# adaLN weights of a two-layer diffusion block: the first layer's later rounds wait for its first, and the second layer's run beside the last route

## The chip, the cores and the metric

One core of one Trainium2 chip runs the whole program. The metric is the device time of one execution in microseconds (us), the median of several runs on one chip.

## What is computed

Two layers of a hybrid attention and expert-retrieval block over 512 latent and 256 context tokens, cut to what matters here:

```python
def reference(...):
    s_c, s_cctx = silu(c), silu(c_ctx)
    h_lat, h_ctx = x, ctx                       # 512 and 256 tokens of 1024
    for l in range(2):
        mod = (s_c @ ada_w[l] + ada_b[l]).reshape(1, 6, 1024)
        sh1, sc1, g1, sh2, sc2, g2 = mod
        mod_c = (s_cctx @ ada_w[l] + ada_b[l]).reshape(6, 1024)
        a_lat = rms_norm(h_lat, norm1_g[l]) * (1 + sc1) + sh1
        a_ctx = rms_norm(h_ctx, norm1_g[l]) * (1 + mod_c[1]) + mod_c[0]
        p_lat, p_ctx = a_lat @ w_in[l], a_ctx @ w_in[l]
        o_mla, o_swa = latent attention over ctx and latent keys, windowed attention with sinks
        h_lat = h_lat + g1 * (concat(o_mla, o_swa) @ w_out[l])
        # (layer 0 only: the same for the ctx tokens, which see ctx alone, with mod_c[2])
        b = rms_norm(h, norm2_g[l]) * (1 + sc2) + sh2
        q = (b @ peer_wq[l]).reshape(T, 8, 2, 128);  s = q . peer_keys[l]
        # top 16 of each half, top 16 of the 256 sums: 128 experts idx[t, 8 * 16] per token, softmax g
        a = gelu(b . peer_u[l][idx])
        h = h + g2 * sum_k (g * a)[k] * peer_v[l][idx[k]]
    return h_lat
```

"adaLN" is the line that makes `mod`: two conditioning vectors (latent and context) times a 1024 x 6144 matrix for each layer, 25 MB of float32 a layer, from which come the shifts, scales and gates.

## The kernel before

**How the work is tiled.** Tokens go in tiles of 128: `("ctx", 0..1)` and `("lat", 0..3)`. Each layer has an attention part, in which generators for the steps of a tile are run one after another (`run`) or interleaved by weights (`par`: `par((a, 24), (b, 48))` takes about two steps of b for one of a), and then a dense expert part. The steps: `KV`, `Q`, `KVQ` make keys, values and queries; `A` is attention; `O` the output projection with the gate and the second norm; `R` the route (16 weight tiles `wq` of 512 KB, products L656, scores L631, top 16 by DVE L637 to L641); `G` chooses the experts; `GH` chooses and then builds one-hot tables for a dense tile (`one_hots`: DVE L852 and L863, PE L864, ACT L865, stores `Gd<-ar` from SP). Tiles that are not dense get their experts by gathered rows (`gv<-u,idx`, `gv<-v,idx` by POOL, L766; DVE L770, L780). Of the first layer, the gathers of both context tiles and of latent tile 3 are rows; 353 of these 768 rows are issued ahead of the dense part.

**What sets the order.** Outside the dense loops a scheduler orders each engine's instructions ahead of time; on the chip every engine and every DMA queue takes them strictly in that order. Two buffer pools for weights matter:

- `wts`, tag `w4`: 4 buffers of 512 KB, loaded from SP's queue. All of `w_in`, `wukv`, `w_out`, `wq`, and in the dense part `raw`, pass through them.
- `gat`, tag `gv`: 5 buffers of 512 KB, loaded from POOL's queue. The gathers use them.

**adaLN** (`ada`) takes three rounds a layer. A round loads 16 tiles of 512 KB (8 steps `k`, two tiles each), does 4 products of 2 x 512 for each step (L220, one PSUM bank), loads the bias (`ada_b`, 256 KB), adds it (4 times L226 on DVE), stores the gates of rounds 1 and 2 to memory, transposes (L232) and copies the result out. Round 0 gives `m[0]`, `m[1]` (first norm), round 1 the first gate and `m[3]`, round 2 `m[4]` and the second gate. Round 0 of the first layer uses `w4` from SP; all other rounds use `gv` from POOL and the one PSUM bank `acc` (tag `acc`, one buffer), which `one_hots` needs too (L829, L830). The first layer's three rounds are all free to start at once. The second layer's three start when the queries of context tile 1 exist (`early`), that is beside `A(ctx 1)`, `R(ctx 0)` and the latent `KV`:

```python
a = ada(l, m)
next(a)
run(KVQ(c, 0, 1))
run(a, A(c, 0), O((c, 0)))
early = qs[c, 1][1][:, 0, 0:1]
par((A(c, 1), 16), (R((c, 0)), 16))
run(G(c, 0), ada(1, mods[1], early))
...
par((R((t, 3)), 24), (GH(2, True), 48))
run(G(t, 3))
```

The functions that the diff touches:

## Time and profile before

| | us |
|---|---|
| median of 3 runs | 4384.81 |
| lowest, highest run | 4382.21, 4393.07 |
| profiled execution | 4393.17 |
| its span on the core | 4391.4 |

The profiled execution lies 8.4 us above the median, and its own time is 1.8 us more than its span. All positions below are microseconds from the start of that span. PE is TensorE (matmul), PEld its weight loads, DVE VectorE, ACT ScalarE, POOL GpSimd, SP SyncE; "SPq" and "POOLq" are queues. A fp32 product counts as two records (x8 is four products).

### The profile page before, as it was taken

What the parts mean: (1) busy time and instruction counts of PE and PEld (TensorE: products, weight loads), DVE (VectorE), ACT (ScalarE), POOL (GpSimd) and SP (SyncE); (2) the same over time, 40 slices, a digit from 0 to 9 for tenths busy, and PEclk for the clock granted to TensorE, in tenths of its full rate; (3) what the DMA queues carried; (4) which work ended last, traced back from release to release, by engine and by line L of the source; (5) the groups of instructions that cost most, each with busy time, mean ns of one, the idle gap of its engine ahead of it and who ended that gap; (6) DMA issues with size and microseconds to landing.
All of it is one profiled execution on the core that took longest, in us unless ns stands there. A gap on an engine that the chain in (4) does not pass through costs nothing.

```text
span 4391.4 us, 58196 instructions
## 1 busy us (share of the span) xinstructions
PE 3604.6 (82%) x19934; PEld 2903.4 (66%) x19934; DVE 3370.1 (77%) x7630; ACT 1658.4 (38%) x3116; POOL 1632.5 (37%) x1402
## 2 busy tenths in 40 slices
PE   6886679478786999999999678677776469999997
PEld 2453348347576899999999545444555357888886
DVE  1247778989778888888888743578889989888887
ACT  1332232146465333333333234142223554444443
POOL 2015564554200444444444510155454444222222
PEclk8997789688898999999999889888888569999999
DMA  8488898888746999999999862689899889999997
GB/s 305 161 295 295 308 336 320 299 294 320 249 166 219 352 336 336 337 354 336 336 335 316 317 223 87 212 311 365 292 341 339 279 295 394 317 322 318 319 319 245
DMA packets 471066, 1306.51 MB, mean 298 GB/s; under 512 B 45152, under 2 KB 151392, under 8 KB 470768
## 3 DMA queue, kind: packets, MB, share of 16 engines
q0 software_dynamic: 199744, 726.26, 46.6%
q1 hardware_dynamic: 271024, 576.52, 37.6%
q8 instruction: 157, 2.57, 0.2%
q14 instruction: 141, 1.16, 0.1%
HBM read 1240.70 MB, written 61.90 MB: 297 GB/s over the span
## 4 chain that ended last, share of the span: by engine, by line
PE 27%; DVE 24%; issue 22%; DMA 13%; ACT 7%; POOL 6%; POOLq 0%; ACTq 0%; SPq 0%; DVEq 0%
DVE vacc L780 6%; POOL gv L766 6%; PE m L656 4%; DVE gv L770 4%; DVE v L880 3%; PE A L943 3%; PE o L906 3%; DMA gv<-v,idx 3%; ACT u L879 3%; PE m L384 3%; DMA gv<-u,idx 2%; DMA w<-w_in 2%; PE acc L864 2%; PE big L587 1%; DMA raw<-uT 1%
## 5 line engine op out<-in xcount | busy, mean ns | idle before, releaser
L766 POOL DMA_INDIRECT gv<-v,idx x640 | 777.6, 1215 | 1105.8 <-DVE vacc L780 757.1
L766 POOL DMA_INDIRECT gv<-u,idx x640 | 792.5, 1238 | 863.2 <-DVE a L770 511.7
L943 PE MATMUL A<-b,u 128*128 128x384 f32 (+1 forms) x6144 | 960.4, 312 | 55.0 <-ACT w L946 28.2
L943 PEld LDWEIGHTS A<-b,u 128*128 128x128 f32 x6144 | 929.6, 191 | 91.7 <-ACT w L946 46.1
L906 PE MATMUL o<-v,W 128*128 128x512 f32 x3840 | 922.5, 392 | 9.5 <-ACT W L879 9.5
L780 DVE SCALAR_TENSOR_TENSOR vacc<-gv,a,vacc 128x1024 f32<-128x1024 f32 x635 | 811.5, 1278 | 54.3 <-DMA gv<-v,idx 47.0
L770 DVE CUSTOM_DVE_ANT_0 gv<-gv,btok 128x1024 f32<-128x1024 f32 x640 | 768.9, 1219 | 86.2 <-DMA gv<-u,idx 83.6
L906 PEld LDWEIGHTS o<-v,W 128*128 128x128 f32 x3840 | 713.2, 189 | 148.3 <-ACT W L879 10.0
L880 DVE TENSOR_TENSOR u<-raw,u 128x1024 fp32r<-128x1024 f32 x256 | 313.6, 1225 | 116.0 <-ACT u L879 114.0
L879 ACT ACTIVATE W<-w 128x384 fp32r<-128x384 f32 (+1 forms) x256 | 120.9, 472 | 711.9 <-DVE w L949 711.9
L384 PE MATMUL m<-w,aT 128*128 128x256 f32 (+3 forms) x672 | 256.8, 531 | 86.5 <-DMA w<-w_in 53.5
L880 DVE TENSOR_TENSOR v<-raw,v 128x1024 fp32r<-128x1024 f32 x256 | 312.2, 1219 | 17.4 <-ACT v L879 17.3
L656 PE MATMUL m<-bT,wq 128*128 128x128 f32 x2432 | 304.5, 282 | 3.1 <-DMA wq<-wq 2.5
L656 PEld LDWEIGHTS m<-bT,wq 128*128 128x128 f32 x2432 | 292.6, 199 | 7.3 <-DMA wq<-wq 3.4
L879 ACT ACTIVATE v<-raw 128x1024 fp32r<-128x1024 f32 x256 | 268.3, 1048 | 24.3 <-PE o L906 23.8
L879 ACT ACTIVATE u<-raw 128x1024 fp32r<-128x1024 f32 x256 | 267.7, 1046 | 25.5 <-DMA raw<-uT 25.3
L384 PEld LDWEIGHTS m<-w,aT 128*128 128x128 f32 x672 | 139.6, 218 | 188.9 <-DMA w<-w_in 66.6
L946 ACT ACTIVATE w<-A 128x384 f32<-128x384 f32 (+1 forms) x256 | 109.2, 426 | 354.7 <-PE A L943 354.7
L880 DVE TENSOR_TENSOR W<-w,W 128x384 fp32r<-128x384 f32 (+1 forms) x256 | 125.8, 491 | 143.7 <-ACT W L879 143.6
L516 ACT ACTIVATE peT<-m 128x512 f32<-128x512 f32 (+1 forms) x192 | 109.8, 576 | 238.3 <-PE m L519 132.3
L548 PE MATMUL big<-kT,qT 96*128 96x256 f32 (+1 forms) x288 | 135.8, 606 | 72.8 <-ACT pexp L496 35.0
L864 PE MATMUL acc<-o,o 128*128 128x128 f32 x768 | 140.1, 336 | 65.7 <-ACT ar L865 60.7
(223 smaller groups left out, 4347.8 us busy)
## 6 DMA issues: line engine op xcount, KB each, us to landing
raw<-uT SPq DMA_DIRECT2D x256, 512.0 KB, 5.5
raw<-v SPq DMA_DIRECT2D x256, 512.0 KB, 5.4
wq<-wq SPq DMA_DIRECT2D x136, 512.0 KB, 6.6
gv<-ada_w POOLq DMA_DIRECT2D x80, 512.0 KB, 6.7
Gd<-ar SPq DMA_DIRECT2D x80, 512.0 KB, 4.1
w<-w_out SPq DMA_DIRECT2D x68, 512.0 KB, 6.2
G<-Gd SPq DMA_DIRECT2D x128, 192.0 KB, 5.8
G<-Gd SPq DMA_DIRECT2D x128, 128.0 KB, 5.5
```

Of the source, the lines that this page charges most:

```text
L384: nc.tensor.matmul(ps[:, :cn], aT[:, k, :], w[k][:, :cn], start=(k == 0), stop=(k == KC - 1))
L516: nc.scalar.activation(dv, pt[:, :2 * bn * P], AF.Copy)
L548: nc.tensor.matmul(ps[:, k0:k0 + n], qT[:, h, :], kv["kT"][:, h, k0:k0 + n], start=True, stop=True)
L656: nc.tensor.matmul(ps[:, c], w[:, k, :], bT[:, k, :], start=(k == 0), stop=(k == KC - 1))
L766: return t, nc.gpsimd.indirect_dma_start(out=t, out_offset=None, in_=src, in_offset=bass.IndirectOffsetOnAxis(ap=idx[:, k:k + 1], axis=0))
L770: ins = nc.vector.tensor_tensor_reduce(out=t, in0=t, in1=bt, scale=1.0, scalar=0.0, op0=OP.mult, op1=OP.add, accum_out=a[:, k:k + 1])
L780: return nc.vector.scalar_tensor_tensor(acc, t, w[:, k:k + 1], acc, op0=OP.mult, op1=OP.add)
L864: nc.tensor.matmul(ps[:, x * NK:(x + 1) * NK], o1[:, x], o2, start=True, stop=True)
L879: nc.scalar.activation(hi, x, AF.Copy)
L880: nc.vector.tensor_tensor(lo, x, hi.bitcast(F32), OP.subtract)
L906: nc.tensor.matmul(acc[t][x], W[:, a_, c], v[:, b_, x * 512:(x + 1) * 512], start=(e == 0 and (a_, b_) == PARTS[0]), stop=(e == NK - 1 and ...
L943: nc.tensor.matmul(A, u[:, a_, k * P:(k + 1) * P], b[:, b_, k], start=(k == 0 and (a_, b_) == PARTS[0]), stop=(k == KC - 1 and (a_, b_) == ...
```

## The change

Two edits. In the first layer, the first tile of round 1 is written by a DVE copy of round 0's result (L205), so its load, and all of POOL's loads behind it, wait for round 0. The second layer's three rounds leave the place beside context route 0 and run as a third member of the last `par` of layer 0, beside the route of latent tile 3 and the one-hots of latent tile 2; their weights and biases go through `w4` from SP, and their gates are stored from ACT's queue.

```diff
--- before.py
+++ after.py
@@ -201,7 +201,7 @@
             ws = []
             for i in range(2):
                 w = gv_tile(2 * 512).rearrange("p (j n) -> p j n", j=2)
-                if after is not None and (r, k, i) == (0, 0, 0):
+                if after is not None and (k, i) == (0, 0):
                     nc.vector.tensor_copy(w[:, 0, 0:1], after)
                 nc.gpsimd.dma_start(w.rearrange("p j n -> p (j n)"),
                                     I["ada_w"][l][k * P:(k + 1) * P, (2 * r + i) * D:(2 * r + i + 1) * D])
@@ -209,24 +209,30 @@
             return ws
         return load
 
-    def ada(l, m, early=None):
+    def ada(l, m):
+
 
         for r in range(3):
-            load, ps_a, ps_t = (ada_w, mm, m1) if (l, r) == (0, 0) else (ada_w_early(early), acc_ps, acc_ps)
+            late = l > 0
+            load, ps_a, ps_t = (ada_w, mm, m1) if (l, r) == (0, 0) else \
+                (ada_w, acc_ps, acc_ps) if late else (ada_w_early(m[0][:, 0, 0:1] if r == 1 else None), acc_ps, acc_ps)
+            q = nc.sync if late else nc.gpsimd
             ps = ps_a()
             for k in range(KC):
                 w = load(l, r, k)
                 for j in range(4):
                     nc.tensor.matmul(ps[32 * j:32 * j + 2, :], sT[:, k, :], w[j],
                                      start=(k == 0), stop=(k == KC - 1))
-            rows = gv_tile(512)
-            nc.gpsimd.dma_start(rows, I["ada_b"][l, r])
+                if late:
+                    yield
+            rows = wts.tile([P, 512], F32, tag="w4", name="adab") if late else gv_tile(512)
+            q.dma_start(rows, I["ada_b"][l, r])
             for j in range(4):
                 x = rows[32 * j:32 * j + 2, :]
                 nc.vector.tensor_tensor(x, x, ps[32 * j:32 * j + 2, :], OP.add)
                 i = 2 * r + j // 2
                 if i in (2, 5):
-                    nc.gpsimd.dma_start(gates[l, i][:, (j % 2) * 512:(j % 2 + 1) * 512], x)
+                    (nc.scalar if late else q).dma_start(gates[l, i][:, (j % 2) * 512:(j % 2 + 1) * 512], x)
             pt = ps_t()
             for c in range(4):
                 nc.tensor.transpose(pt[:, c * P:(c + 1) * P], rows[:, c * P:(c + 1) * P], ident)
@@ -1083,9 +1089,8 @@
                 next(a)
                 run(KVQ(c, 0, 1))
                 run(a, A(c, 0), O((c, 0)))
-                early = qs[c, 1][1][:, 0, 0:1]
                 par((A(c, 1), 16), (R((c, 0)), 16))
-                run(G(c, 0), ada(1, mods[1], early))
+                run(G(c, 0))
                 run(KV(t, 0, 1), KV(t, 2, 3), Q(t, 0, 1), A(t, 0), O((c, 1), (t, 0)))
                 par((A(t, 1), 8), (R((c, 1), (t, 0)), 24))
                 run(G(c, 1), O((t, 1)), Q(t, 2, 3))
@@ -1093,7 +1098,7 @@
                 run(O((t, 2)))
                 par((A(t, 3), 8), (R((t, 2)), 24), (GH(1), 48))
                 run(O((t, 3)))
-                par((R((t, 3)), 24), (GH(2, True), 48))
+                par((R((t, 3)), 24), (GH(2, True), 48), (ada(1, mods[1]), 40))
                 run(G(t, 3))
             else:
                 run(KV(c, 0, 1), KV(t, 0, 1), Q(t, 0), left)
```

How it moves instructions, at three places. PE at the start (`m_136` is round 0's PSUM bank, `acc` that of the other rounds; `gv` and `adaw` are weight tiles, `sT` the conditioning vectors, `hld` a token tile). Before:

```order
L220 MATMUL acc<-gv,sT 2x512 x4
L220 MATMUL m_136<-adaw,sT 2x512 x4
L220 MATMUL acc<-gv,sT 2x512 x2
L220 MATMUL m_136<-adaw,sT 2x512 x4
L220 MATMUL acc<-gv,sT 2x512 x6
```

PE at the start now (line numbers of the changed kernel: L224 is L220, L238 is L232, L283 is L277, L390 is L384):

```order
L224 MATMUL m_136<-adaw,sT 2x512 x32
L238 MATMUL m_207<-ident,gv 128x128 x4
L283 MATMUL m_229<-diag,hld 128x128 x4
L283 MATMUL m_238<-diag,hld 128x128 x4
L390 MATMUL m_283<-w_275,aT 128x288 x2
```

Round 0's 32 products stand alone at the head; round 1's follow behind the first norm, and round 1 now ends (its L232) where round 2 ended before, round 2 some 30 us of the old timeline later, behind the query projection.

POOL's queue, from the first load to the first gathers. Before:

```order
L206 DMA gv<-ada_w 128x1024 x16
L223 DMA gv<-ada_b 128x512
L206 DMA gv<-ada_w 128x1024 x14
L796 DMA btok<-b_ctx_1151 128x1024
L206 DMA gv<-ada_w 128x1024 x2
L223 DMA gv<-ada_b 128x512
L206 DMA gv<-ada_w 128x1024 x4
L229 DMA gate_92<-gv 2x512 x2
L206 DMA gv<-ada_w 128x1024 x12
L223 DMA gv<-ada_b 128x512
L229 DMA gate_93<-gv 2x512 x2
L766 DMA gv<-u,idx 128x1024 x128
```

These are the second layer's 48 loads; the first layer's 32 stand ahead of them. Now, from the first load of all on:

```order
L229 DMA gv<-ada_b 128x512
L206 DMA gv<-ada_w 128x1024 x16
L229 DMA gv<-ada_b 128x512
L206 DMA gv<-ada_w 128x1024 x4
L235 DMA gate_90<-gv 2x512 x2
L206 DMA gv<-ada_w 128x1024 x12
L229 DMA gv<-ada_b 128x512
L235 DMA gate_91<-gv 2x512 x2
L802 DMA btok<-b_ctx_1152 128x1024
L772 DMA gv<-u,idx 128x1024 x128
```

The second layer's loads are gone from it.

SP's queue at the last route (`b_lat` is the stored second norm of tile 3, which is ready only when that norm is). Before:

```order
L182 DMA w_8011<-w_out 128x2x512
L652 DMA wq<-wq 128x1024 x4
L248 DMA gate<-gate_90 128x512
L868 DMA Gd<-ar 128x1024 x2
L152 DMA h_lat_8033<-hld 128x1024
L613 DMA b_lat_8074<-hld 128x1024
L652 DMA wq<-wq 128x1024 x4
L868 DMA Gd<-ar 128x1024
L652 DMA wq<-wq 128x1024 x3
L868 DMA Gd<-ar 128x1024
```

Now:

```order
L193 DMA adaw<-ada_w 128x1024 x2
L874 DMA Gd<-ar 128x1024
L193 DMA adaw<-ada_w 128x1024 x2
L254 DMA gate<-gate_90 128x512
L874 DMA Gd<-ar 128x1024
L152 DMA h_lat_7783<-hld 128x1024
L874 DMA Gd<-ar 128x1024
L658 DMA wq<-wq 128x1024
L193 DMA adaw<-ada_w 128x1024 x4
L619 DMA b_lat_7824<-hld 128x1024
L658 DMA wq<-wq 128x1024
L193 DMA adaw<-ada_w 128x1024 x2
```

Between one `wq` tile and the next stand two to four `adaw` tiles; 58 tiles for `w4` and 16 of the `Gd` stores follow behind `b_lat`, the last `wq` behind the last `Gd`. On PE the one-hots' first step (`acc<-ident,ef`) stands behind the 32 products of the second layer's round 0, since both use the bank `acc`.

## Rows read from the trace of the kernel before

**Rows 1.** The page, busy time of each engine over the whole span (share, instructions).

```profile
PE 3604.6 (82%) x19934; PEld 2903.4 (66%) x19934; DVE 3370.1 (77%) x7630; ACT 1658.4 (38%) x3116; POOL 1632.5 (37%) x1402
```

**Rows 2.** Stretches: PE, PEld, DVE, ACT, POOL busy (instructions); clock, DMA share, GB/s.

```profile
0.00:60.00 60.00, 34.04 (x137) 4.59 (x138) 6.10 (x21) 5.56 (x9) 11.83 (x28) 0.77 0.95 356
108.00:175.00 67.00, 50.07 (x157) 29.25 (x158) 11.89 (x29) 23.44 (x53) 0.00 (x0) 0.89 0.38 128
175.00:347.00 172.00, 148.13 (x941) 88.07 (x940) 79.50 (x399) 63.51 (x171) 27.31 (x53) 0.95 0.73 253
347.00:1240.00 893.00, 653.58 (x3646) 471.69 (x3647) 734.22 (x1994) 329.67 (x743) 431.07 (x358) 0.82 0.85 301
1275.00:1409.00 134.00, 87.79 (x624) 79.25 (x623) 107.20 (x477) 74.65 (x136) 0.57 (x1) 0.84 0.63 213
1409.00:2400.00 991.00, 988.20 (x4991) 899.81 (x4991) 845.93 (x1140) 359.44 (x484) 454.14 (x353) 1.00 0.95 336
```

**Rows 3.** The same view, line L220 alone (PE busy, PEld busy, clock, DMA).

```profile
60.00:108.00 48.00, 13.21 (x64) 1.52 (x64) 0.96 0.70 238
...
175.00:250.00 75.00, 19.02 (x100) 2.15 (x100) 0.91 0.76 258
...
175.00:347.00 172.00, 35.66 (x192) 4.11 (x192) 0.95 0.73 253
```

**Rows 4.** Timeline, start and first gather: start, duration, engine, line, tile, count [idle before].

```profile
4.34 2.09 SPq L193 DMA_DIRECT2D adaw<-ada_w  x4
...
7.16 3.62 PE L220 MATMUL acc<-gv,sT 128*2 128x512 f32 x8 [7.16 <-DMA gv<-ada_w]
...
54.36 1.69 PE L220 MATMUL m<-adaw,sT 128*2 128x512 f32 x8
...
103.88 0.66 PE L232 MATMUL acc<-ident,gv 128*128 128x128 f32 x4
...
346.97 1.07 POOL L766 DMA_INDIRECT gv<-u,idx  x1 [6.78 <-issue]
```

**Rows 5.** DMA of 0 to 60 us: GB/s in 40 slices, issues with landing time.

```profile
GB/s 0 71 239 398 409 257 280 325 413 423 418 423 414 414 395 420 416 421 418 426 415 418 426 418 421 350 281 268 232 300 396 415 426 415 421 361 225 329 358 370
...
adaw<-ada_w SPq DMA_DIRECT2D x16, 512.0 KB, 9.9
```

**Rows 6.** Chain that ended last, 175 to 250 us, by line; waits 175 to 347 us.

```profile
by line: issue 22.7%; PE big L587 19.0%; PE acc L220 14.4%; DMA gate<-gate 13.3%; DMA gv<-ada_w 11.1%; PE m L277 5.0%; PE m L519 2.4%; PE m L512 2.0%; ACT L253 1.7%; PE big L565 1.7%; DVE upd L596 1.6%; ACT upd L261 1.5%; PE big L548 1.4%; 
...
PE acc L232 <- DVE gv L226: 3.1, 1, 3.1
```

**Rows 7.** DMA of 1275 to 1409 us: packets and bytes, issues with landing time.

```profile
DMA packets 16660, 28.58 MB, mean 213 GB/s; under 512 B 1190, under 2 KB 10406, under 8 KB 16650
...
wq<-wq SPq DMA_DIRECT2D x16, 512.0 KB, 4.6
...
gate<-gate SPq DMA_DIRECT2D x1, 256.0 KB, 4.5
```

**Rows 8.** Timeline of the last route: SP's queue, then PE.

```profile
1304.24 6.58 SPq L652 DMA_DIRECT2D wq<-wq  x4
...
1327.31 4.05 SPq L652 DMA_DIRECT2D wq<-wq  x3
...
1389.71 11.57 SPq L917 DMA_DIRECT2D G<-Gd  x16
...
1299.86 0.42 PE L829 MATMUL acc<-ident,ef 128*128 128x128 f32 x1
...
1408.67 1.01 PE L943 MATMUL A<-b,u 128*128 128x384 f32 x2 [22.80 <-ACT u L879]
```

**Rows 9.** Timeline of DVE there, and line L226's durations (min/median/max ns).

```profile
1384.22 0.34 DVE L863 TENSOR_SCALAR o<-io,i,gT 128x128 f32<-128x128 f32 x1
...
1385.26 0.28 DVE L641 FIND_INDEX8 i<-v,mrep 128x8 uint32<-128x128 f32 x1
...
L226 DVE TENSOR_TENSOR gv<-gv,acc x12: 668/683/694, 218.9 to 338.7; 2x512 f32<-2x512 f32 x12
```

## The prediction

> **What bounds the kernel now.** I began with the page's busy times. No engine holds the whole span: PE has 82%, DVE 77% [rows 1]. So I cut the span into stretches and read for each which column is nearest to full [rows 2]. The reader should see six different kernels there. The dense stretch (1409 to 2400) is PE-bound, 988 of 991 us, and the change leaves its instructions alone; it moves as a block. The gather stretch (347 to 1240) has no full engine: DVE is busy 734 of 893 us and the DMA share is 0.85. The edits touch the other four: the first 60 us, where the DMA share is 0.95 and PE waits for weights; 108 to 175, where PE has 17 us idle and the DMA is at 0.38; 175 to 347, where PE is busy 148 of 172 us; and the last route, 1275 to 1409, where PE is busy 88 of 134 us, DVE 107, and the DMA share is 0.63. In the first stretch I read the timeline [rows 4] and the transfers [rows 5]; in 175 to 347 the chain and the waits [rows 6]; at the last route the transfers and the timelines [rows 7 to 9].
>
> **Part 1a: round 0 alone at the start.** Rounds 0 and 1 load together, and the last product of round 0 is at 54.4 us, ending at 56 [rows 4]. The stretch moves 356 GB/s on average, 413 to 426 in its best slices, and an `adaw` tile takes 9.9 us to land in this crowd [rows 5]. Alone, round 0 needs its 16 tiles and what else is loaded beside it (two token tiles and small tables, which I take as 3 tiles more): 19 x 0.524 = 10 MB. At 356 GB/s that is 28 us. It starts when the first tile lands: issue at 4.3 [rows 4] and, with the queue empty, about 5 us as the 4.6 of a `wq` tile in a quieter place [rows 7]. 9 + 28 = 37 us instead of 56: **-19 us**. Bounds: at 418 GB/s 24 us and an end at 33, -23; if four buffers starve and the rate falls to 300 (the 301 of the gather stretch, rows 2), 33 us and an end at 42, -14.
>
> **Part 1b: rounds 1 and 2 come later.** Round 1's first load in POOL's queue now waits for the result of round 0, and everything of POOL behind it: the other 31 tiles, the bias loads, the gate stores. That is 16 MB from about 38 us, at 356 GB/s done by 85 us, so the transfers are not late for what follows. The products are in another place, though: round 1's stand where round 2's stood (64 records, 13.2 us of PE between 60 and 108, rows 3), and round 2's 13.2 us go behind the query projection, into 108 to 175. There PE has 17 us of idle time [rows 2], but a chain of attention steps and norms goes through it, and an idle share of 25% does not hide all of it. I take two thirds, **+9 us**. Bounds: 0 if PE's idle time takes it; 20 if all 13.2 count and the bank `acc`, the adds (4 x 0.68 us, rows 9) and the gate make the second norm late by some 7 us more.
>
> **Part 2a: the second layer's rounds leave 175 to 347.** In 175 to 250 us the chain gives 14.4% of 75 us, 10.8 us, to L220 [rows 6], and L220 was busy there for 19.0 us [rows 3]: 57% of it was on the path. Of the 35.7 us in the whole stretch [rows 3] that is 20.3. The chain also has 13.3%, 10 us, on a gate load [rows 6] that takes 4.5 us where there is less traffic [rows 7]: 5.5 more. A transposition that waits 3.1 us for an add [rows 6] goes too. **-29 us**. Bounds: 9 if only the two waits go and other work fills the 35.7 us; 44 if all of it was on the path. Parts 1 and 2a together bring POOL's first gather from 347.0 [rows 4] to about 308.
>
> **Part 2b: the same work beside the last route.** It adds 48 weight tiles of 0.524 MB and three biases to a stretch that moves 28.58 MB [rows 7]: 28.6 + 26.0 = 54.5 MB. All of it and the 16 `wq` tiles go through the 4 `w4` buffers in SP's order, and 58 tiles stand behind the store `b_lat`, which waits for tile 3's second norm. What waits behind SP's waiting instruction: the route's `wq` tiles and 16 `Gd` stores. What waits behind round 0 on PE: the first step of the one-hots, which needs the bank `acc`. I cost it along that order. Before, the first `wq` behind `b_lat` goes at 1304.2 and the one-hots' first product at 1299.9 [rows 8]. Now 12 tiles of round 0 come behind `b_lat`: 12 x 1.5 us (1.5 is what a tile takes at 356 GB/s), the last lands 4.6 us after its issue [rows 7], and four adds take 2.7 [rows 9]: 1304.2 + 18 + 4.6 + 2.7 = 1329.5, so the one-hots begin about 29 us late. They took from 1299.9 [rows 8] to 1384.2 [rows 9] on a DVE that was busy 107 of 134 us [rows 2], so little of a late start is made up; eight more adds of rounds 1 and 2 put 5.5 us on it. At the end the last `wq` now stands behind the last `Gd`, and on DVE the last top-16 and the choice of tile 3 come after the last one-hot, where they were over 1 us behind it before [rows 9]: a landing of 4.6, a product and the searches, 10 us. 29 + 5.5 + 10 = **+45 us**. Read the other way this is 58 tiles at 2.0 us each: 1304 + 116 + 10 = 1430 against 1385.
>
> Bounds of this term come from the bytes. 54.5 MB take 130 us at the 418 GB/s of the best early slices [rows 5], within the old 134: +0, hidden. At 356 they take 153, +19; at 336 (the dense stretch, rows 2) 162, +28; at 301 (gathers) 181, +47. I chose a value near the last, since stores in small packets (10,406 of 16,660 under 2 KB, rows 7) and waits in one queue mix here as among the gathers, and not as at the start. PE could hold it: 87.8 + 35.7 = 123.5 us of work in 134.
>
> Rows 5 show slices of 413 to 426 GB/s for more than 20 us in a stretch of loads from memory. The Trainium skill, page "DMA: Bandwidth & Descriptors", section "Where 436 GB/s comes from", says that for transfers between memory and SBUF the memory's side, about 358 GB/s for a core, is what binds. The measurement goes above that here, so it decides for the bound of +0; by the page's figure the stage would need an estimated 152 us, +18, and the sum would be 21 us below the old time.
>
> **Sum.** -19 + 9 - 29 + 45 = **+6 us**. On the profiled execution's 4393.2 (span 4391.4 and 1.8 around it) that is 4399; this execution lay 8.4 us above the median, so against the median of 4384.8 I forecast **4391 us**. A measurement of this kernel tells about 0.3%, 13 us, from no change: 4371.7 to 4398 is "same".
>
> **Rivals.**
> *A, faster: the tail has room.* The last route's DMA ran at 213 GB/s with a share of 0.63 [rows 2], PE and DVE have 46 and 27 us free, and 16 tiles landed in 4.6 us each [rows 7]. If the mixed queue keeps 356 GB/s, the stage grows by 19 only: -39 + 19 = -20, **4365 us**. For it: three engines with room. Against it: the order in one queue behind one store.
> *B, slower: the ring of four starves.* In the old route the 12 `wq` tiles behind `b_lat` took from 1304.2 to 1331.4 [rows 8], 2.26 us each, paced by the products that free the buffers. If all 58 go at that pace (131 us), and the bank `acc` stops the ring at each of three rounds for four adds, the transposition and a copy (about 4.4 us, 13 in all), the last tile goes at 1304 + 144 = 1448 and the choice ends at 1458 instead of 1385: +73. -39 + 73 = +34, **4419 us**. It decides once a tile costs more than about 2.2 us. For it: PE order is strict, so a late `adaw` tile also holds the one-hots and the route behind it. Against it: `adaw` tiles are used by 8 short records, and free their buffer quickly.
> *C, slower: the front gives little.* The work taken out of 175 to 347 could be filler: the chain has 22.7% "issue" [rows 6], and other PE work may have been what the next step waited for. Then part 2a is its lower bound of 9 and the sum +26, **4411 us**.
> That the weights of the second layer were free where they stood, in a word C with a hidden tail (+0), would be -19 + 9 - 9 = -19, and falls with A.
>
> **How the numbers follow.** The forecast, within 0.3%, has 38%; A 27%; B 25%; C 10%. So faster 0.27, same 0.38, slower 0.35. The likeliest case is 4391, its own range 4372 to 4398. The 8-in-10 range must reach both A and B: 4362 (A and a few us of part 1) to 4424 (B and a few us); outside are a hidden tail with the full front gain (-39, 4346) and B together with C (4439).
>
> **What the profile would show.** Part 1a: the last `m<-adaw` product at about 37 us. 1b: round 2's transposition by 125 us, and no new wait for it in the chain. 2a: the first gather near 308; the stretch from there to the end of the rows as long as before, 893 us. 2b: the first one-hot product some 29 us later, counted from the end of tile 3's output projection; about 300 GB/s in the last route; the first dense product, 1408.7 before [rows 8] behind the loads of `G` that began at 1389.7, at about 1414; and the dense stretch again 991 us. I am wrong if the first gather does not move by at least 30 us, if the tail's rate is over 340 or under 270 GB/s, or if the gather stretch changes its length.

## The result, and the profile after

The changed kernel takes 4440.8 us (median of 4 runs, 4440.2 to 4450.6) against 4388.1 of before on the same chip: a ratio of 1.013, 95% interval 1.011 to 1.015. It is slower by some 53 us, and outside the forecast range (4362 to 4424). The profiled execution has a span of 4448.9 us.

The windows of the changed kernel, cut where the work of [rows 2] now lies (us; PE, PEld, DVE, ACT, POOL busy and their instructions; the granted clock of TensorE as a share of full speed; the DMA share, which is the mean busy share of the core's DMA engines; GB/s):

```profile
0.00:60.00 60.00, 34.56 (x160) 14.25 (x164) 6.52 (x27) 12.74 (x30) 6.50 (x17) 0.94 0.79 278
108.00:175.00 67.00, 54.40 (x196) 28.69 (x195) 14.22 (x31) 24.14 (x55) 3.69 (x7) 0.90 0.38 124
175.00:319.00 144.00, 114.84 (x723) 85.15 (x722) 69.14 (x377) 55.15 (x158) 0.98 (x2) 0.89 0.42 137
319.00:1212.00 893.00, 642.90 (x3627) 461.96 (x3625) 729.92 (x1981) 325.30 (x733) 433.66 (x358) 0.83 0.85 301
1250.00:1442.00 192.00, 136.85 (x831) 86.24 (x830) 114.15 (x476) 80.12 (x139) 0.57 (x1) 0.86 0.84 282
1442.00:2433.00 991.00, 987.23 (x4986) 898.45 (x4986) 846.60 (x1149) 358.51 (x483) 455.31 (x352) 1.00 0.96 336
```

The stretch ahead of the gathers is 28 us shorter and its DMA share fell from 0.73 to 0.42; the gather and dense stretches read as before. The last route's window is 58 us longer (192 against 134), at 282 GB/s. That is above every bound of part 2b, of which the dearest had 181 us.

The PE timeline at the start of the changed kernel (start, duration, engine, line, tile, count [idle before]): the last product of round 0, the transposition that follows it, and round 2's.

```profile
39.11 1.03 PE L224 MATMUL m<-adaw,sT 128*2 128x512 f32 x4 [1.16 <-DMA adaw<-ada_w]
43.02 0.69 PE L238 MATMUL m<-ident,gv 128*128 128x128 f32 x4 [2.88 <-DVE gv L232]
...
129.69 0.60 PE L238 MATMUL acc<-ident,gv 128*128 128x128 f32 x4
```

Its first gather on POOL, 347.0 before [rows 4]:

```profile
318.57 1.01 POOL L772 DMA_INDIRECT gv<-u,idx  x1 [90.73 <-PE m L380]
```

SP's queue at the last route of the changed kernel, from the `b_lat` store to the dense loads:

```profile
1277.78 0.33 SPq L619 DMA_DIRECT2D b_lat<-hld  x1
1278.94 0.33 SPq L658 DMA_DIRECT2D wq<-wq  x1
1279.90 0.82 SPq L193 DMA_DIRECT2D adaw<-ada_w  x2
1281.37 0.33 SPq L658 DMA_DIRECT2D wq<-wq  x1
1288.39 3.79 SPq L193 DMA_DIRECT2D adaw<-ada_w  x4
...
1404.49 0.33 SPq L658 DMA_DIRECT2D wq<-wq  x1
1405.92 10.09 SPq L903 DMA_DIRECT2D raw<-bT  x12
1423.83 11.38 SPq L923 DMA_DIRECT2D G<-Gd  x16
```

The last `wq` goes out 127 us behind `b_lat`; before, the last ended 28 behind it. PE at the end of that stretch:

```profile
1404.86 1.03 PE L224 MATMUL acc<-adaw,sT 128*2 128x512 f32 x4 [0.40 <-DMA adaw<-ada_w]
1406.15 1.03 PE L224 MATMUL acc<-adaw,sT 128*2 128x512 f32 x4 [0.27 <-DMA adaw<-ada_w]
1410.08 1.11 PE L238 MATMUL acc<-ident,adab 128*128 128x128 f32 x4 [2.90 <-DVE adab L232]
1410.98 3.62 PE L662 MATMUL m<-bT,wq 128*128 128x128 f32 x16
1415.29 2.07 PE L637 MATMUL m<-keys,pq 128*128 128x128 f32 x8 [0.69 <-ACT pq L668]
1441.62 1.01 PE L949 MATMUL A<-b,u 128*128 128x384 f32 x2 [24.25 <-ACT u L885]
```

The route's last product stands on PE behind round 2's last tiles, four adds and a transposition. Its scores are there at 1417; on DVE the last top 16 ends at 1423.7, 27 us behind the last one-hot (1396.8), and only then do the `G` loads start. The 58 tiles for `w4` behind `b_lat` went out from 1278.9 to 1404.5, 2.16 us each (2.07 in the second profile, `again`).

Two profiles of each kernel (the second ones are the runs `before_again` and `again` below) give the account, in us:

| | before, two executions | changed, two executions | difference of means |
|---|---|---|---|
| first gather | 347.0, 344.8 | 318.6, 317.3 | -27.9 |
| from there to the `b_lat` store of tile 3 | 956.0, 949.2 | 959.2, 956.8 | +5.4 |
| from `b_lat` to the first dense product | 105.7, 104.3 | 163.8, 156.3 | +55.1 |
| dense stretch, to the second layer's first norm | 1101.9, 1102.6 | 1104.6, 1105.7 | +2.9 |
| from there to its second dense stretch | 1090.7, 1078.9 | 1115.6, 1100.5 | +23.3 |
| rest of the span | 790.1, 790.3 | 787.0, 789.8 | -1.8 |

The sum is +57 us; by their medians the two kernels are 48 to 53 us apart. Two executions of one kernel are up to 22 us apart in the span, so terms below some 10 us are not to be read from one profile.

### The profile page after: what moved, and what is told of

It is laid out like the page before. It is cut to its first block, busy times and chain, and to the rows that moved or that the text cites. A ratio compares the mean times of both kernels' runs of the same rounds, so it can differ in the third digit from the quotient of the medians.

```text
span 4448.9 us, 58204 instructions
## 1 busy us (share of the span) xinstructions
PE 3621.8 (81%) x19934; PEld 2902.6 (65%) x19934; DVE 3371.4 (76%) x7630; ACT 1657.2 (37%) x3112; POOL 1600.0 (36%) x1347
## 4 chain that ended last, share of the span: by engine, by line
PE 41%; DVE 23%; issue 13%; DMA 12%; ACT 8%; POOL 3%; SPq 0%; ACTq 0%; POOLq 0%; DVEq 0%
PE A L949 10%; PE o L912 10%; DVE vacc L786 5%; DVE gv L776 5%; PE m L662 4%; DVE v L886 3%; POOL gv L772 3%; ACT u L885 3%; DMA gv<-u,idx 3%; PE m L390 2%; PE acc L870 2%; DMA gv<-v,idx 2%; PE m L518 1%; PE m L525 1%; PE big L593 1%
## 5 line engine op out<-in xcount | busy, mean ns | idle before, releaser
L886 DVE TENSOR_TENSOR u<-raw,u 128x1024 fp32r<-128x1024 f32 x256 | 313.6, 1225 | 112.5 <-ACT u L885 104.7
L390 PE MATMUL m<-w,aT 128*128 128x256 f32 (+3 forms) x672 | 262.4, 541 | 88.4 <-DMA w<-w_in 49.7
L390 PEld LDWEIGHTS m<-w,aT 128*128 128x128 f32 x672 | 143.3, 223 | 196.5 <-DMA w<-w_in 62.8
L498 DVE TENSOR_REDUCE nb<-big 128x1 f32<-128x768 f32 (+3 forms) x160 | 122.4, 766 | 99.5 <-PE big L554 48.7
L522 ACT ACTIVATE peT<-m 128x512 f32<-128x512 f32 (+1 forms) x192 | 109.6, 577 | 233.3 <-PE m L518 101.5
```

What stands on the lines that cost most here:

```text
L390: nc.tensor.matmul(ps[:, :cn], aT[:, k, :], w[k][:, :cn], start=(k == 0), stop=(k == KC - 1))
L498: nc.vector.tensor_reduce(nb, ps[:, :n], AX.X, OP.max, negate=True)
L522: nc.scalar.activation(dv, pt[:, :2 * bn * P], AF.Copy)
L886: nc.vector.tensor_tensor(lo, x, hi.bitcast(F32), OP.subtract)
```

## The experiments

Positions, read from each run's timelines, in us; the last five columns count from the `b_lat` store of latent tile 3. "One-hots start" is the product `acc<-ident,ef`, "last `wq`" the end of its issue, "dense start" the first product `A<-b,u`; the last one-hot and the last top 16 are the starts of their last rows on DVE. The intervals are of 95%.

| run | ratio to before, interval | first gather | `b_lat` | one-hots start | last `wq` | last one-hot | last top 16 | dense start |
|---|---|---|---|---|---|---|---|---|
| before | | 347.0 | 1303.0 | -3.1 | 28.4 | 81.2 | 82.3 | 105.7 |
| changed | 1.013 [1.011, 1.015] | 318.6 | 1277.8 | 31.1 | 127.0 | 119.1 | 145.7 | 163.8 |
| wait_only | 0.9991 [0.9977, 1.0005] | 339.3 | 1286.6 | -3.4 | 28.3 | 79.2 | 80.3 | 103.5 |
| move_only | 1.0109 [1.0075, 1.0142] | 318.7 | 1279.2 | 25.3 | 120.3 | 112.3 | 137.4 | 155.7 |
| own_sp | 1.0093 [1.0067, 1.012] | 313.1 | 1284.0 | 38.8 | 32.4 | 129.7 | 109.6 | 157.2 |
| own_pool | 1.0074 [1.0051, 1.0097] | 316.7 | 1285.2 | 40.4 | 31.3 | 128.1 | 124.9 | 157.8 |
| late_8 | 1.0101 [1.0065, 1.0137] | 318.0 | 1285.4 | -3.1 | 107.6 | 88.9 | 121.7 | 158.5 |
| own_late_8 | 1.0107 [1.0087, 1.0126] | 313.5 | 1272.0 | -4.5 | 38.5 | 103.3 | 86.6 | 167.2 |
| half_bytes | 1.007 [1.0043, 1.0097] | 315.0 | 1283.5 | 21.0 | 101.8 | 131.3 | 132.2 | 155.5 |
| third_pe | 1.0111 [1.0079, 1.0143] | 314.0 | 1265.6 | 31.7 | 124.8 | 122.2 | 141.9 | 160.3 |
| third_half | 1.0072 [1.0049, 1.0095] | 310.1 | 1269.8 | 22.3 | 93.6 | 116.7 | 118.7 | 140.8 |
| late_third_half | 1.0044 [1.0027, 1.0061] | 312.2 | 1266.0 | -3.1 | 77.1 | 99.5 | 102.6 | 129.6 |
| own_late_third_half | 1.0033 [1.0017, 1.0049] | 313.4 | 1274.0 | -4.1 | 37.1 | 101.9 | 101.2 | 125.5 |
| none | 0.9989 [0.9968, 1.0009] | 314.9 | 1281.4 | -3.1 | 28.4 | 80.3 | 81.3 | 105.2 |
| mid_8 | 1.0059 [1.0042, 1.0076] | 315.8 | 1319.2 | -3.1 | 28.4 | 81.1 | 82.2 | 104.8 |
| old_w4 | 1.0159 [1.0142, 1.0177] | 316.6 | 1344.9 | -3.1 | 28.4 | 81.0 | 82.1 | 104.5 |
| weight_36 | 1.0077 [1.0057, 1.0098] | 315.1 | 1266.2 | 30.2 | 109.8 | 120.0 | 127.4 | 151.3 |
| weight_48 | 1.0111 [1.0076, 1.0145] | 317.4 | 1273.5 | 27.8 | 119.5 | 113.7 | 135.5 | 153.9 |
| again | 1.0133 [1.0116, 1.015] | 317.3 | 1274.1 | 26.3 | 121.3 | 112.5 | 138.3 | 156.3 |
| before_again | 1.0003 [0.999, 1.0016] | 344.8 | 1294.0 | -3.1 | 28.4 | 81.1 | 82.2 | 104.3 |

**One edit at a time.** In wait_only the kernel before gets the first edit alone.

```diff
-                if after is not None and (r, k, i) == (0, 0, 0):
+                if after is not None and (k, i) == (0, 0):
```

with `after` the result of round 0 for the first layer's round 1.

> The kernel before with the first edit alone (round 1 of the first layer waits for round 0; the second layer's rounds stay beside context route 0, through gv). Front theory (each edit has its own share of the front gain): round 0 ends near 40 us as in the changed kernel, the first attention output about 10 us earlier, the second layer's rounds still on the path between 175 and 347, so the first gather near 337 instead of 347 and the total about 10 us below before (ratio 0.998). Rival (the whole front gain needs the second edit): first gather within 3 us of 347, total unchanged. On the second layer: if its extra 24 us come with the moved rounds, its part of the trace, from the last product of the first dense stretch to the first of the second, is as long as before, 1146 us within 6; if they come with any change of order, it is off by 10 us or more here too.

The gather came 8 us earlier (5 against the second profile of before), the first output projection 4 (193.1 against 196.8), and the total did not move measurably.

```profile
339.29 1.06 POOL L766 DMA_INDIRECT gv<-u,idx  x1 [6.78 <-issue]
```

In move_only round 1 does not wait:

```diff
-(ada_w_early(m[0][:, 0, 0:1] if r == 1 else None), acc_ps, acc_ps)
+(ada_w_early(None), acc_ps, acc_ps)
```

> The changed kernel without the wait of round 1 (second edit alone). Theory of the ring (the last route's 58 tiles pass the four w4 buffers in one order, so that the last wq lands late): the last route is stretched by about 60 us as in the changed kernel, from the b_lat store to the last top 16 near 146 us instead of 82; the front gives some 17 us less the first edit's share; total 40 to 65 us above before (1.009 to 1.015). Rival (the tail's loss comes from the first edit's changed timing): the tail is stretched by less than 40.

```profile
318.68 1.01 POOL L772 DMA_INDIRECT gv<-u,idx  x1 [86.84 <-PE m L380]
```

The second edit alone gives the whole front gain (318.7) and the loss at the last route: 155.7 us, beside 163.8 and 156.3 in the changed kernel's two profiles. The first edit adds nothing to it.

**Is it the w4 buffers or SP's queue?** In own_sp the second layer's tiles lie in three slices of `v` (the latent values, dead by then), the bias in `sv`; in own_pool POOL's queue issues them. The rounds so leave the four `w4` buffers to the route, but pass a ring of their own, of three.

```diff
-            w = wts.tile([P, 2, 512], F32, tag="w4", name="adaw")
+            n = (2 * (KC * r + k) + i) % 3
+            w = vb["v"][:, 2 * n:2 * n + 2, :] if l else wts.tile([P, 2, 512], F32, tag="w4", name="adaw")
```

> The changed kernel, but the second layer's weight tiles lie in three slices of the latent value tensor (free after the last attention) and the biases in another dead tensor: the same bytes, products, bank and queue (SP), but w4 is left to the route. Ring theory: the route's tiles no longer stand behind adaLN tiles in a buffer, the last wq is issued within 45 us of b_lat instead of 127, the last top 16 comes with the last one-hot, and the dense start is at least 25 us earlier than the changed kernel's (33 us after before's): at most +8. Rival of the bytes and PE (54.5 MB and 36 us of products more make the stage that long wherever they lie): the stage from b_lat to the last top 16 stays within 10 us of 146.

> As own_sp, but the second layer's tiles are issued from POOL's queue, which has nothing else there. If SP's strict order is a part of the loss beside the buffers, the dense start is another 5 us or more earlier than in own_sp; if only the buffers matter, the two are within 5 us; if bytes or PE set the stage, it stays within 10 us of 146 in both.

The ring theory falls as the reason for the dense start. The route did come free (last `wq` 31 to 32 behind `b_lat`), and the dense start did not. The one-hots stood behind round 0 at the bank and started 39 and 40 us behind `b_lat`, 42 and 44 later than before. The rounds ended later still: their last product ended 135 us behind `b_lat` in both, 5 and 7 behind the last one-hot, and the loads of `G` waited for the last `Gd` store and, longer, for the gate stores that release `sv` (own_sp, SP's queue from 1415 to 1426: us in total, times, longest):

```profile
SPq L926 <- DMA gate<-sv: 2.7, 2, 2.0
SPq L926 <- DMA Gd<-ar: 2.2, 1, 2.2
```

What a ring costs the rounds themselves these runs don't show, since they have one of three buffers. The queue made no difference in the stage (157.2 and 157.8). The Trainium skill, page "Trainium Kernel Development and Optimization", section "Key Constraints", says that transfers issued from SP, ACT and POOL run on the same 16 DMA engines and that several issuers save issue time alone; these two runs agree.

**Is it the bank?** In late_8 the one-hots go first; own_late_8 has the edits of own_pool too.

```diff
-par((R((t, 3)), 24), (GH(2, True), 48), (ada(1, mods[1]), 40))
+par((R((t, 3)), 24), (GH(2, True), 48), (later(8, ada(1, mods[1])), 40))
```

(`later` yields eight times ahead of its generator.)

> The changed kernel with eight empty steps ahead of the moved rounds, so that the one-hots' first step takes the bank acc before round 0 does; the weights still pass w4. Theory of the bank: the one-hots start within 6 us of the place they had before (3 us ahead of the b_lat store, in the changed kernel 31 behind it) and the last one-hot is at most 95 us behind b_lat (119 in the changed kernel, 81 before); the w4 order still puts the last wq late, so the last top 16 is over 110 behind b_lat and the dense start gains less than 25. Rival (bytes, PE and DVE work make the stage long, whoever goes first): the last one-hot stays over 110 us behind b_lat.

> Both: the moved rounds in their own slices from POOL's queue, and eight empty steps ahead of them. If the bank and the w4 order are the two causes, each hiding the other (own_pool freed the route and the one-hots were last; late_8 frees the one-hots), the dense start is at most 125 us behind b_lat (106 before, 164 in the changed kernel, 158 in own_pool) and the total falls below before, to some 4360 to 4380. Rival of the bytes and of PE: still over 145 us.

The bank moves the one-hots as expected (-3.1, last 88.9), and the dense start stays. The rounds themselves were last in late_8: their last product ended 144 us behind `b_lat`, 22 behind the last top 16. With route and one-hots both freed (own_late_8) it ended 145 us behind `b_lat`, and the dense start came at 167; there the rounds also hold `v`, and the loads of `G` waited 33.6 us for it (SP's queue from 1360 to 1450):

```profile
SPq L926 <- DMA v<-ada_w: 33.6, 1, 33.6
```

Three chains, and whichever is let go, another ends about as late. The windows of own_late_8, from `b_lat` to the last one-hot and from there to the last adaLN product, show two reasons:

```profile
1272.00:1376.00 104.00, 94.69 (x643) 65.01 (x641) 76.12 (x335) 53.52 (x96) 15.29 (x29) 0.97 0.89 306
1376.00:1417.00 41.00, 24.74 (x80) 3.10 (x80) 16.64 (x76) 3.73 (x4) 7.91 (x15) 0.75 0.70 233
```

In the first PE is busy 91% and the DMA share is 0.89: something that the chains share is near full. In the second the rounds run alone, PE at 60% and the DMA share at 0.70, and on POOL's queue 11 of 13 issues wait for a product to free one of the three slices. There the small ring of this edit is the likely pace, so the 167 us, over the 145 stated, speak neither for nor against the bytes and PE. A kernel with more buffers was not run.

**Bytes or TensorE?** half_bytes loads half of each tile of the moved rounds (`w[:, :1, :]`, and both products of the tile read it); third_pe makes one of four products after a round's first step; third_half does both.

```diff
-                    nc.tensor.matmul(ps[32 * j:32 * j + 2, :], sT[:, k, :], w[j],
-                                     start=(k == 0), stop=(k == KC - 1))
+                    if not late or k == 0 or j == 0:
+                        nc.tensor.matmul(ps[32 * j:32 * j + 2, :], sT[:, k, :], w[j],
+                                         start=(k == 0), stop=(k == KC - 1 or (late and j > 0)))
```

> The changed kernel, each weight tile of the moved rounds loaded to its half (256 KB), the other half's products made with the same half: 12.6 MB less in the last route, the same tiles in w4, products, bank. It leaves the true values out. Theory of the bytes: 12.6 MB at 281 GB/s are 45 us, the stage from b_lat to the dense start shrinks from 164 to 135 or less. Theory of the orders (bank and w4): within 12 us of 164, since tiles are waited for by landing and use, not by rate.

> The changed kernel with 33 of the 96 products of the second layer's rounds (after the first step of a round one of four): all bytes, tiles and banks, but about 12.4 instead of 36 us of TensorE. It leaves the true values out. Theory of TensorE (from b_lat to the last top 16 it was busy 82% before, and 82% of 133 us with half the bytes, so that the stage grows by its added work over 0.82): 23.6 us less work make the stage from b_lat to the dense start 20 to 30 us shorter than the changed kernel's 164. Theory of the transfers: within 10 us of 164, since every tile still has to land in the same order. The second layer has nearly the changed kernel's order here (10 rows differ), so by the theory of the order it takes over 1158 us again.

> third_pe and half_bytes together: 12.4 us of products and half the bytes. It leaves the true values out. If TensorE alone sets the stage, as in third_pe, 134 to 144; if transfers and TensorE replace each other as the limit (taking one away alone bares the other), it falls well below both, to 115 to 130 us; if neither matters but the order of the rounds, it stays over 150.

Each alone did nothing that can be told from the spread: 155.5 and 160.3, where five profiles with all the work there (changed, again, move_only, weight_36, weight_48) lie from 151 to 164. Both together gave 140.8, 16 to 23 us below the changed kernel's two profiles and 10 below the lowest of the five. By the ranges stated, half_bytes came out as the theory of the orders had it, and third_pe as that of the transfers. third_half missed the range of two limits (115 to 130) and lies in that of TensorE alone (134 to 144), which does not fit, since third_pe did not shorten the stage. But third_pe is a weaker test than it was meant to be: its products kept 29.1 us of PE, not 12.4 (last section). The windows from `b_lat` to the last top 16 suggest why. Before:

```profile
1303.00:1386.00 83.00, 68.50 (x539) 65.62 (x538) 66.59 (x266) 53.92 (x100) 0.00 (x0) 0.92 0.59 203
```

The changed kernel:

```profile
1278.00:1424.00 146.00, 114.03 (x723) 72.32 (x721) 79.03 (x293) 58.67 (x101) 0.00 (x0) 0.91 0.84 282
```

half_bytes:

```profile
1284.00:1416.00 132.00, 108.55 (x705) 73.43 (x704) 78.04 (x292) 54.83 (x99) 0.00 (x0) 0.92 0.66 219
```

third_pe:

```profile
1266.00:1407.00 141.00, 103.38 (x605) 75.04 (x604) 77.66 (x288) 58.79 (x100) 0.00 (x0) 0.87 0.83 291
```

Before, PE was busy 68.5 of 83 us, 83%, in this stage. With half the bytes the DMA share falls to 0.66 and PE is at 82% again. With fewer products PE falls to 73% and the DMA share stays at 0.83. So one of the two stays where it was while the other is eased: two limits that stand close together, and a stage with little room for either. This is argued from the shares and from third_half. It is not shown that PE or the transfers alone set a length: in half_bytes PE still waited 12.2 us for `wq` tiles, and own_late_8 ran at 91% for 104 us.

**The bank and the rest.** late_third_half is third_half with late_8's eight steps; own_late_third_half also has own_pool's slices and queue.

> third_half with eight empty steps ahead of the rounds (one-hots first at the bank, a third of the products, half the bytes; the true values are left out). third_half still had the one-hots 25 us late behind round 0 and the dense start 141 us behind b_lat. If the bank's order is what remains, the one-hots start 3 us ahead of b_lat as before and the dense start comes 105 to 118 us behind it; if it is the mixture in SP's queue, it stays over 130.

> late_third_half with the rounds out of w4 and out of SP's queue (slices of the latent values, POOL's queue; a third of the products, half the bytes, true values left out). In late_third_half the dense start was still 130 us behind b_lat (105 without the rounds), the last wq issued 77 behind it instead of 28. If what remains is the mixture with the route's tiles in w4 and SP's queue, the last wq comes 28 to 35 behind b_lat and the dense start 105 to 115; if it is the rest of bytes and products, it stays over 122.

late_third_half came to 129.6, from 140.8, between its two stated ranges: the bank's order is a part once the two limits are eased. Its window:

```profile
1266.00:1369.00 103.00, 90.03 (x605) 66.29 (x605) 72.50 (x276) 54.66 (x99) 0.00 (x0) 0.98 0.81 274
```

own_pool and late_8, which had freed the route or the one-hots alone, stood at 84% and 86%. own_pool:

```profile
1285.00:1414.00 129.00, 108.44 (x703) 68.92 (x701) 75.31 (x294) 54.51 (x100) 22.19 (x42) 0.97 0.87 297
```

late_8:

```profile
1285.00:1407.00 122.00, 105.14 (x707) 68.01 (x705) 72.62 (x275) 59.38 (x102) 0.00 (x0) 0.99 0.89 308
```

In late_third_half PE is at 87%, and its busy time is 21.5 us above before's; the window is 20 longer. own_late_third_half had the last `wq` 37.1 behind `b_lat` and still the dense start at 125.5: over 122, so the queue mixture is not what remains.

In steps, from the changed kernel's 160 us (mean of its two profiles) down to the 105 without the rounds (none, below): 19 us go with half the bytes and a third of the products, 11 with the bank's order, 4, no more than executions differ by, with the queue and `w4`. The last 20 go with the rest of the rounds and are not split further.

**What the rounds cost at each place.** none leaves the second layer's rounds out:

```diff
-                par((R((t, 3)), 24), (GH(2, True), 48), (ada(1, mods[1]), 40))
+                par((R((t, 3)), 24), (GH(2, True), 48))
```

> The changed kernel without the second layer's three rounds: the second layer uses the first layer's shifts, scales and gates, so its values are not the true ones. It prices the rounds at each place by a floor. Theory (the rounds cost 22 to 30 us at the old place and 45 to 60 at the last route or in the gather stage): first gather at 310 to 320, the last route as before (dense start 100 to 108 us behind b_lat), total 22 to 32 us below before, 4350 to 4360. Rival (the old place hid them, and the front gain of the changed kernel comes from somewhere else): total within 12 us of before.

```profile
1281.00:1363.00 82.00, 66.25 (x542) 63.74 (x542) 66.23 (x265) 53.90 (x100) 0.00 (x0) 0.96 0.59 206
```

The stage, whose window this is, was the old one, the gather at 315, but the total only 0.1% below before (interval from 0.3% below to 0.1% above): there was at most 0.3% to win. mid_8 puts the rounds, through w4, beside the second latent attention tile; old_w4 beside context route 0, through w4:

```diff
-par((A(t, 1), 8), (R((c, 1), (t, 0)), 24))
+par((A(t, 1), 8), (R((c, 1), (t, 0)), 24), (ada(1, mods[1]), 8))
```

```diff
-                run(G(c, 0))
+                run(G(c, 0), ada(1, mods[1]))
```

> A version that may beat both: the second layer's rounds through w4 and SP, but in the par of the second latent attention tile with the routes of context tile 1 and latent tile 0 (weight 8), inside the gather stage, where TensorE has 73% and the DMA share is 0.85, and no one-hots need the bank acc. Theory: the front keeps its gain of about 28 us, the last route is the old one (dense start 106 us behind b_lat), and the added 36 us of TensorE and 25 MB cost the gather stage part of their length: 10 to 40 us; total 4365 to 4395. Rival (the rounds cost the same wherever they pass w4): about 55 us more in that stage, total near 4410.

> The changed kernel with the second layer's rounds back beside context route 0, but through w4 and SP's queue as in the change. Theory of the place (what counts is how full the transfers are: share 0.73 there with the rounds in it, 0.85 in the gather stage): first gather at 340 to 352, total within 12 us of before. Theory of the ring (passing w4 among a route's tiles costs 45 us or more wherever it is): first gather at 360 or later, total 20 us or more above before.

In both the last route was the old one. old_w4 had its last adaLN product at 399.5. Against none's `b_lat` at 1281.4 the rounds cost 38 us in mid_8 and 63 in old_w4. At old_w4's place, but through gv, they cost 5 (wait_only, 1286.6) or 13 and 22 (the two executions of before); executions differ by some 10. So both theories stated for old_w4 missed a part: the gathers were not held up, but the work after 317 us was. In mid_8 the 38 us lie in the range stated, but its median of 4405.8 us is above 4365 to 4395 and nearer to the rival's 4410. No version beat before.

**The second layer.** weight_36 and weight_48 have 36 and 48 in place of the weight 40. With 36, TensorE's order in the second layer is before's; with 48 the changed kernel's.

> The changed kernel with the weight of the moved rounds in the last par 36 instead of 40. The order of TensorE in the second layer is then the one of the kernel before (no row differs; 188 rows differ in the changed kernel), while the last route keeps its kind of mixture. Theory of the order (the changed kernel's extra 26 us in the second layer come from the other order that the scheduler chose there): the second layer takes 1140 to 1148 us instead of 1166, the dense start is within 8 us of the changed kernel's 1442, and the total is 15 to 25 us below the changed kernel. Rival (transfers that happen to fall otherwise on the chip): the second layer still takes over 1158.

> The changed kernel with weight 48 instead of 40: another mixture at the last route (190 rows of TensorE), but in the second layer row for row the order of the changed kernel. Theory of the order: the second layer takes over 1158 us as in the changed kernel (1166), against 1138 to 1147 in all kernels so far with the old order. Rival (chance of the transfers): under 1150.

> The changed kernel once more, unchanged. In weight_48 the second layer's TensorE order is the changed kernel's row for row, and still the layer took 1093 us from its first norm to its second dense stretch, as in all others (1086 to 1099), not 1116. If those 25 us were chance of one execution, this profile shows 1086 to 1100 there, and the total comes nearer to the 4426 of move_only and weight_48. If they belong to this kernel's order on DVE and ACT, the layer takes over 1108 again and the total stays near 4440.

> The kernel before once more, unchanged. Kernels whose order ahead of the last route is nearly the same had their b_lat store between 17.6 and 37.4 us ahead of the one of before, so one execution can lie some 10 us off in the gather stage. If the first profile of before was a slow one (its 4391.4 us lay 8 above the median), this one has its first gather within 3 us of 347 but b_lat 5 to 15 us earlier than 1303, and the front gain of the change shrinks to 10 to 20 us, as the 5 us by which leaving the rounds out lowers the median suggest. Otherwise b_lat is at 1303 within 4 us.

From the layer's first norm to its second dense stretch (the expectations of weight_36 and weight_48 count from an earlier event) weight_36 took 1092.2 us, which seemed to bear the theory of the order out, though its dense start came 24 us earlier than the changed kernel's and not within 8. weight_48 took 1092.7 with the other order: the theory falls. again took 1100.5, its median is 4431.8; before_again 1078.9, at 4383.7, with `b_lat` 9 us earlier. The first profiles of both kernels lay at the upper end of their kernel's runs.

## Why the prediction was wrong

Between the forecast's +6 us and the account's +57 lie 51 us: 11 in the front (-39 forecast, -28 measured), 5 in the gather stretch, 10 at the last route (+45, +55), 3 in the dense stretch and 23 in the second layer, less 2 in the rest. The step that failed by most is a term that the sum did not have.

**The second layer was in no part of the sum.** The forecast took it as unmoved and gave no reason, and it is 23 us longer in the mean of two profiles each. Two profiles of one kernel differ there by 12 and 15 us, so the size is uncertain. TensorE's order is not the cause (weight_48). In the other kernels it took 1086 to 1116: 1097.7 in none, and 1116.3 in own_late_third_half, so length like the changed kernel's comes with other last routes too. The windows of the changed kernel's first profile and of before_again:

```profile
2546.00:3662.00 1116.00, 765.03 (x4081) 560.07 (x4081) 810.78 (x2369) 399.70 (x866) 396.02 (x348) 0.79 0.76 269
2501.00:3580.00 1079.00, 739.40 (x4081) 544.44 (x4082) 806.70 (x2366) 397.83 (x866) 395.66 (x347) 0.81 0.78 278
```

The work is the same; PE was busy 765 us at a granted clock of 0.79, and 739 at 0.81. Over all twenty profiles the layer took 1079 to 1098 us where this mean clock was 0.81 and 1095 to 1116 where it was 0.79. That goes with the length; what lowers the clock, and whether the change does, stays open.

**Parts 1 and 2a: each came out, their sum did not.** Round 0 ends at 40.1 (42.1 in again) instead of 56; the forecast was 37. Part 1 as a whole was forecast at -10, and the first edit alone brought the gather 7.7 us earlier (wait_only). Part 2a was forecast at -29, and the second edit alone brought it 28.3 us earlier (move_only). Both together gave 28.4. Adding the two as if they were independent is the step that failed in the front. Why part 1's share is lost when the second layer's rounds are gone was not followed up. The sign named for this came up: the gather moved by less than 30 us.

**Part 2b failed in size and in its reason.** +45 became +55 (58 and 52 in the two pairs of profiles). Its first term was right: the one-hots start 34 and 29 us later against `b_lat`, forecast 29. The 12 tiles counted there are eight of round 0, three of the route and the bias. The second term, 5.5 us for eight adds, fits too: the one-hots took 88 and 86 us instead of 84. The third did not: "a landing of 4.6, a product and the searches, 10 us" measured 27 and 26 from the last one-hot to the last top 16, 1 before. It did not count that the last product waits on PE behind round 2's last tiles, their adds and the transposition. 5 us came back: the dense start follows the last top 16 in 18 us, 23 before. The rate gave no warning: 282 GB/s lie within the 270 to 340 that were stated.

The reason under it was wrong as well. "PE could hold it: 87.8 + 35.7 = 123.5 us of work in 134" was read from a window [rows 2] that has the 23 us of dense setup in it, when PE has nothing to do. In the stage itself PE was busy 68.5 of 83 us. The products were 44.6 us of PE there, not 35.7:

```profile
1260.00:1420.00 160.00, 44.59 (x192) 4.13 (x192) 0.90 0.84 286
```

(line L224 alone, PE and PEld busy, clock, DMA). PE's busy time grew by 45.5 us in the two windows from `b_lat` to the last top 16; at the old 83% an estimate from that alone is 55 us. The transfers grew as well: share times window is 49 us before and 123 in the changed kernel.

**Rival A** falls: there was no room. **Rival B** had +73 for the stage, more than the measured +55. Its pace for a tile, 2.26 us, is about as near to the measured 2.16 and 2.07 as the forecast's 2.0; its stops at the bank did not add their 13 us. Its reason is half tested: freeing the route of the ring (own_sp, own_pool) did not shorten the stage, but no run gave the rounds more buffers. Without the second layer the account comes to +34, which is B's sum; that is luck, since B has both its front and its last route too large. **Rival C** is right that the front gives less (-28, between its -19 and the forecast's -39), but not in its reason: the rounds taken out were worth what 2a said. Why the `w4` buffers make the rounds dear beside context route 0, where `gv` does not, stays open.

## What to carry to other kernels

Read a stage's room between the two events that bound it, not in a window with idle ends: here that raised PE's share from 66% to 83%, and the kernels with work added ran at 73 to 91%. Where two limits lie close (here PE at 83% and a DMA share that rises to 0.84 with the added bytes), a run that eases one can show nothing; ease both, and price the work by leaving it out altogether. Do that first: none shows that the place to be improved held at most 0.3%. And price two edits of one path alone and together before their gains are added.

## What was not expected of the hardware

A product of 2 x 512 that stands alone holds PE about as long as four of one step that stand together. In the changed kernel a step's four products (eight records) took 1.04 us where both of its tiles had landed, and two took 1.03; in third_pe one took 1.02:

```profile
1389.14 1.04 PE L224 MATMUL acc<-adaw,sT 128*2 128x512 f32 x8
1390.83 1.03 PE L224 MATMUL acc<-adaw,sT 128*2 128x512 f32 x4
...
1391.46 1.02 PE L225 MATMUL acc<-adaw,sT 128*2 128x512 f32 x2
```

So a third of the products kept 29.1 of 44.6 us of PE (66 records of line L225), and 192 records took 35.7 us in the old place [rows 3] and 44.6 at the last route, where they stand more scattered and the granted clock was 0.90 against 0.95. The busy time of PE in a stage is no fixed price of its work.

Two profiles of the same program were 21 us apart (4391.4 and 4370.1, at mean granted clocks of 0.892 and 0.900), spread over the gather stage and the second layer.
